# Twelve of 22 gate and up pairs of each FFN from seven block products, and the FFN in three blocks

## The chip, the cores and the metric

The kernel runs on one core of a Trainium2 chip, in one launch. The metric is the device time of that launch in microseconds. TensorE (PE) does the matrix products; its weight loads (PEld) are listed apart from its products. VectorE (DVE), ScalarE (ACT) and GpSimd (POOL) work element by element, and SyncE (SP) issues the loads of the weights from memory.

## The reference

One decoder layer on 512 tokens of width D = 1024, all in fp32. Its first and its last stage are the same kind of feed-forward network (FFN), each with its own weights; the token mixers and a cross-attention between them are not touched by the change.

```python
def swiglu(u, w_gate_up, w_down):
    gate, up = jnp.split(u @ w_gate_up, 2, axis=-1)
    return (jax.nn.silu(gate) * up) @ w_down

h = h + 0.5 * swiglu(rmsnorm(h, g1), w_gu1, w_d1)     # w_gate_up: 1024 x 5632, w_down: 2816 x 1024
...                                                   # mixers, cross-attention
h = h + 0.5 * swiglu(rmsnorm(h, g2), w_gu2, w_d2)
out = rmsnorm(h, g_final)
```

The width of the FFN, 2816, is 22 chunks of 128 (KF = 22); the width of the model is 8 chunks (KD = 8).

## The kernel before

All values lie transposed: 128 features of a chunk on the partitions, the 512 tokens along the row. A product of one 128x128 block of weights with a chunk's 512 tokens is one accumulation step. To keep fp32's accuracy, each fp32 operand is held as two numbers of the faster type fp32r, a rounded one ("hi") and the rest ("lo"), and each step is three products: hi by hi (L114), hi by the tokens' lo (L115), the weights' lo by hi (L116). `split` makes the two: ScalarE casts (L88), then VectorE subtracts (L89).

`load_w` brings 1024 columns of weights (eight blocks of 128) with one DMA into `wr` and splits them into `wh` and `wl`; each of the three names is a ring of three buffers. `job(pt, w, xs)` loads the weights of one output chunk and runs its products into one PSUM tile: 24 of them for eight input chunks, 66 (three loads of 1024, 1024 and 768 columns) for 22. PSUM has five buffers `pj` for such outputs and three `ss` for small things.

`ffn` goes over the 22 chunks `ct`. For each it runs two jobs, one for the gate (`pg`) and one for the up projection (`pu`), 48 products of 512 tokens. Then VectorE multiplies `pg` by the norm's factor `r` (L181), ScalarE takes silu (L182), VectorE multiplies by `pu` (L183), and the result is split into `sh` and `sl`, which stay for all 22 chunks. After the 22nd come eight down jobs of 66 products over all of them; each is scaled (L197) and added to `h` (L199). In the second FFN the last down job is `finish`: in two halves of 256 tokens it does the 66 products (L654 to L656), the final norm, the transposes and the output's DMA.

The tokens' own factors are `uh` and `ul` (`gained`, L123 and L124: h times the norm's gain, split). The order of the instructions on each engine comes from a scheduler that works from the order of the code, and each engine then runs its list in that order, waiting where a semaphore is not there yet.

Of the kernel before, what the change touches and what calls it, by code (L numbers as in the profile page):

```python
# [46 lines left out]
def layer(ctx: ExitStack, tc: tile.TileContext, a, out):  # L48
# [120 lines left out]

    def ffn(gname, wgu, wd, fin=None):  # L170
        with tc.tile_pool(name=nm("fp"), bufs=1, reuse_waits="tile") as fp:
            u = [gained(h[k], gname, k, up) for k in range(KD)]
            s = []
            for ct in range(KF):
                pg, pu = ps(), ps()
                job(pg, wgu[ct], u)
                job(pu, wgu[KF + ct], u)
                if ct == 0:
                    r = rms(h, D, wk)
                gt = fp.tile([P, T], F32, tag="gt", name=nm("gt"), bufs=2)  # L180
                V.tensor_tensor(out=gt, in0=pg, in1=r, op=ALU.mult)  # L181
                S.activation(out=gt, in_=gt, func=AF.Silu)  # L182
                V.tensor_tensor(out=gt, in0=pu, in1=gt, op=ALU.mult)  # L183
                hi = fp.tile([P, T], F32R, tag=f"sh{ct}", name=nm("sh"))
# [567 lines left out]
```

## Time and profile before

| | us |
|---|---|
| median of 3 runs | 1611.11 |
| lowest and highest | 1610.34, 1614.96 |
| the profiled execution, its own time | 1613.93 |
| its span in the trace | 1612.2 |
| TensorE busy in it | 1583.2 (98%) |
| weight loads busy | 1305.2 (81%) |
| VectorE busy | 853.6 (53%) |
| ScalarE busy | 660.3 (41%) |

The span is what the trace covers; the execution's own time is 1.7 us more, for what lies around it. "Busy" sums the instructions of an engine; weight loads run beside products. The two FFNs take the stretches from the start to about 370 us and from about 1180 us to the end.

### The profile page before, as it was taken

To read this page: it belongs to the slowest core of one execution; us is meant where nothing else is said; L and a number is where in the kernel's file an instruction comes from. 1 tells how busy PE (TensorE), PEld (TensorE's weight loads), DVE (VectorE), ACT (ScalarE), POOL (GpSimd) and SP (SyncE) were. 2 spreads that over 40 slices of the span, in tenths; PEclk is the share of its full clock that TensorE was granted. 3 is DMA by queue.
4 is the path that set the end of the run, shared out by engine and by line. 5 is a ranking of instruction groups with operands and counts; after the bars stand their busy time and mean duration, and the time that the engine had idled before them with its cause. 6 is when DMAs were issued, how large, how long until landed. Compare 5 with 4: busy or idle time off the path is not lost.

```text
span 1612.2 us, 18647 instructions
## 1 busy us (share of the span) xinstructions
PE 1583.2 (98%) x7437; PEld 1305.2 (81%) x7437; DVE 853.6 (53%) x1134; ACT 660.3 (41%) x888; POOL 50.8 (3%) x54
## 2 busy tenths in 40 slices
PE   8999999999999999999999999999999999999997
PEld 6888888887878787787888888888888888888887
DVE  5434343346695877858564544555555434443333
ACT  6223232225778493765332223344443323222222
POOL 0000000000120100201010000000000000000000
PEclk9999999999999999999999999999999999999999
DMA  5332323333442323333253233335213233332331
GB/s 194 94 103 91 103 91 104 115 108 105 126 131 78 125 85 122 114 95 109 85 185 102 92 104 93 94 107 178 79 32 113 92 100 96 94 103 86 95 98 62
DMA packets 53911, 168.58 MB, mean 105 GB/s; under 512 B 6320, under 2 KB 6832, under 8 KB 53824
## 3 DMA queue, kind: packets, MB, share of 16 engines
q1 hardware_dynamic: 51952, 161.03, 32.2%
q0 software_dynamic: 1584, 5.31, 0.9%
q8 instruction: 58, 0.95, 0.2%
q10 hardware_dynamic: 288, 1.05, 0.2%
q14 instruction: 29, 0.24, 0.0%
HBM read 163.10 MB, written 4.26 MB: 104 GB/s over the span
## 4 chain that ended last, share of the span: by engine, by line
PE 57%; issue 1%; DVE 1%; ACT 0%; DMA 0%; DVEq 0%; ACTq 0%
PE pj L114 17%; PE pj L116 17%; PE pj L115 17%; PE pj L520 0%; PE pj L521 0%; PE pj L522 0%; PE ss L383 0%; PE pj L654 0%; PE pj L656 0%; PE pj L655 0%; PE ss L388 0%; DMA m<-acd 0%; PE ss L602 0%; PE ss L565 0%; PE ss L564 0%
## 5 line engine op out<-in xcount | busy, mean ns | idle before, releaser
L88 ACT CAST wh<-wr 128x1024 fp32r<-128x1024 f32 (+2 forms) x298 | 294.3, 988 | 794.2 <-PE pj L115 667.8
L114 PE MATMUL pj<-uh,wh 128*128 128x512 f32 x1416 | 556.4, 393 | 7.0 <-ACT wh L88 7.0
L116 PE MATMUL pj<-uh,wl 128*128 128x512 f32 x1416 | 554.9, 392 | 0.0
L115 PE MATMUL pj<-ul,wh 128*128 128x512 f32 x1416 | 554.3, 392 | 0.0
L89 DVE TENSOR_TENSOR wl<-wr,wh 128x1024 fp32r<-128x1024 f32 (+2 forms) x298 | 341.0, 1145 | 196.9 <-ACT wh L88 190.0
L114 PEld LDWEIGHTS pj<-uh,wh 128*128 128x128 f32 x1416 | 266.6, 188 | 63.2 <-ACT wh L88 7.0
L116 PEld LDWEIGHTS pj<-uh,wl 128*128 128x128 f32 x1416 | 266.5, 188 | 56.9 <-issue 0.7
L115 PEld LDWEIGHTS pj<-ul,wh 128*128 128x128 f32 x1416 | 266.5, 188 | 55.7 <-DVE ul L124 0.7
L114 PE MATMUL pj<-sh,wh 128*128 128x512 f32 x330 | 128.9, 390 | 0.0
L116 PE MATMUL pj<-sh,wl 128*128 128x512 f32 x330 | 128.5, 389 | 0.0
L115 PE MATMUL pj<-sl,wh 128*128 128x512 f32 x330 | 128.5, 389 | 0.0
L183 DVE TENSOR_TENSOR gt<-pj,gt 128x512 f32<-128x512 f32 x44 | 30.4, 691 | 137.2 <-PE pj L116 136.5
L181 DVE TENSOR_TENSOR gt<-pj,r 128x512 f32<-128x512 f32 x44 | 30.3, 691 | 113.0 <-PE pj L116 109.5
L116 PEld LDWEIGHTS pj<-sh,wl 128*128 128x128 f32 x330 | 61.9, 188 | 12.9
L114 PEld LDWEIGHTS pj<-sh,wh 128*128 128x128 f32 x330 | 62.0, 188 | 12.7
L115 PEld LDWEIGHTS pj<-sl,wh 128*128 128x128 f32 x330 | 62.0, 188 | 12.7
L225 DVE SCALAR_TENSOR_TENSOR cv<-cx,prm,cv 128x511 f32<-128x511 f32 (+2 forms) x72 | 63.3, 883 | 3.3 <-ACT cv L222 3.0
L366 POOL TENSOR_TENSOR m<-m,keep 128x512 f32<-128x512 f32 x32 | 40.4, 1277 | 309.9 <-DMA m<-acd 297.6
L116 PE MATMUL pj<-ynh,wl 128*128 128x512 f32 x128 | 49.8, 389 | 0.0
L115 PE MATMUL pj<-ynl,wh 128*128 128x512 f32 x128 | 49.8, 389 | 0.0
L114 PE MATMUL pj<-ynh,wh 128*128 128x512 f32 x128 | 49.8, 389 | 0.0
L138 DVE TENSOR_TENSOR sq<-sq,sq 128x512 f32<-128x512 f32 (+1 forms) x47 | 31.2, 665 | 2.5 <-ACT sq L134 1.8
(223 smaller groups left out, 1661.6 us busy)
## 6 DMA issues: line engine op xcount, KB each, us to landing
wr<-in_w_gu SPq DMA_DIRECT2D x87, 512.0 KB, 3.5
wr<-in_w_in SPq DMA_DIRECT2D x80, 512.0 KB, 3.6
wr<-in_w_d SPq DMA_DIRECT2D x32, 512.0 KB, 3.5
m<-acd SPq DMA_DIRECT2D x32, 256.0 KB, 3.9
wr<-in_w_os SPq DMA_DIRECT2D x32, 256.0 KB, 3.0
wr<-in_w_d SPq DMA_DIRECT2D x16, 384.0 KB, 3.1
ea<-acd SPq DMA_DIRECT2D x32, 128.0 KB, 4.1
wr<-in_w_oa SPq DMA_DIRECT2D x8, 512.0 KB, 3.5
```

The lines of the kernel that those rows point to most:

```text
L88: S.copy(out=hi, in_=src)
L89: V.tensor_tensor(out=lo, in0=src, in1=hi, op=ALU.subtract)
L114: TE.matmul(pt, hi[:, s_], xh, start=(k == 0), stop=False)
L115: TE.matmul(pt, hi[:, s_], xl, start=False, stop=False)
L116: TE.matmul(pt, lo[:, s_], xh, start=False, stop=(k == nk - 1))
L138: V.tensor_tensor(out=sq, in0=acc, in1=sq, op=ALU.add)
L181: V.tensor_tensor(out=gt, in0=pg, in1=r, op=ALU.mult)
L183: V.tensor_tensor(out=gt, in0=pu, in1=gt, op=ALU.mult)
L225: V.scalar_tensor_tensor(out=acc[:, d:], in0=x[:, :T - d], scalar=pc(wname, j0 + j), in1=acc[:, d:], op0=ALU.mult, op1=ALU.add)
L366: G.tensor_tensor(out=m4, in0=m4, in1=acs[:, (h0 + hh) * NC:(h0 + hh + 1) * NC].unsqueeze(2) .to_broadcast([P, NC, P]), op=ALU.subtract)
```

## The change

`ffn` works in three blocks of chunks (SB = 8: chunks 0 to 7, 8 to 15, 16 to 21). Each block is followed by the eight down jobs over its own chunks alone (24, 24 and 18 products each), so `h` is scaled and added to three times instead of once, and `sh` and `sl` are kept for eight chunks.

In each FFN 12 of the 22 chunks (`seven`: 4, 5, 7, 8, 10, 11, 13, 14, 16, 17, 19, 20) get their gate and up projections by Strassen's scheme. The weights of a pair are seen as four blocks (a, c: gate and up over input chunks 0 to 3; b, d: over chunks 4 to 7), the tokens as two halves of 256 times two groups of input chunks, and seven products of such blocks replace eight. Each has four input chunks and 256 tokens, so 12 products of 256 columns: 7 x 12 = 84 products of 256 columns in place of 48 of 512. `seven_a` runs four of the seven (48 products, L212 to L215 in `mm3`), `seven_b` the other three (36), one chunk later in the code. The remaining ten chunks (`plain`) are computed as before.

Around them: `_pairs` packs the weights of a pair in the new order on the host, so the two DMAs of a pair remain 1024 columns each. VectorE forms sums of weight blocks (`s31` in two halves, `ca` in place, `s4`: 512 columns each), and the splits of a pair are three of 1024 columns (`w31`, `w2a`, `wdb`) and one of 512 (`w4`). `token_sums`, once in an FFN behind chunk 1, forms the four sums of token blocks and splits them into `th` and `tl`. At the output, ScalarE copies two halves out of PSUM into `ev` and VectorE adds (L291 and its like), then forms `xx` (L304 to L307) and `gt` (L311, L312). OFF and the tile `lag` shift the places in the local memory of some tiles: read from the built programs, the tokens of a product start at the same address modulo 512 bytes as its weights in nearly all products of before, and 192 bytes past it in the seven-product pairs.

```diff
 NC = 4
 EPS = 1e-6
+def seven(ct):
+    return ct >= 4 and ct % 3 != 0
...
+    def ring(tag, dt=F32R):
+        return wp.tile([P, 1024], dt, tag=tag, name=nm(tag), bufs=3)
...
-    first.append(load_w(a["w_gu1"][KF][:, :8 * P], 8 * P))
+    first.append(load_w(a["w_gu1"][0][:, 8 * P:], 8 * P))
...
     def ffn(gname, wgu, wd, fin=None):
-        with tc.tile_pool(name=nm("fp"), bufs=1, reuse_waits="tile") as fp:
-            u = [gained(h[k], gname, k, up) for k in range(KD)]
-            s = []
-            for ct in range(KF):
-                pg, pu = ps(), ps()
-                job(pg, wgu[ct], u)
-                job(pu, wgu[KF + ct], u)
-                if ct == 0:
-                    r = rms(h, D, wk)
-                gt = fp.tile([P, T], F32, tag="gt", name=nm("gt"), bufs=2)
-                V.tensor_tensor(out=gt, in0=pg, in1=r, op=ALU.mult)
-                S.activation(out=gt, in_=gt, func=AF.Silu)
-                V.tensor_tensor(out=gt, in0=pu, in1=gt, op=ALU.mult)
-                hi = fp.tile([P, T], F32R, tag=f"sh{ct}", name=nm("sh"))
-                lo = fp.tile([P, T], F32R, tag=f"sl{ct}", name=nm("sl"))
-                split(gt, hi, lo)
-                s.append((hi, lo))
+        fs = ExitStack()
+        fp = fs.enter_context(tc.tile_pool(name=nm("fp"), bufs=1, reuse_waits="tile"))
+        ts = ExitStack()
+        tp = ts.enter_context(tc.tile_pool(name=nm("tp"), bufs=1, reuse_waits="tile"))
+        tp.tile([P, 48], F32, tag="lag", name=nm("lag"))
+        u = [gained(h[k], gname, k, up) for k in range(KD)]
+        tq = []
+        s = {}
+        def split_pair(src):
+            ws = [fp.tile([P, 1280], F32R, tag=t, name=nm(t), bufs=2) for t in ("xh", "xl")]
+            split(src.rearrange("p (a n) -> p a n", a=2),
+                  *(t[:, :2 * (512 + OFF)].rearrange("p (a n) -> p a n", a=2)[:, :, :512]
+                    for t in ws))
+            return ws
+        def mm3(pt, w, off, xs, start, stop):
+            hi, lo = w
+            for k in range(4):
+                c = slice(off + k * P, off + (k + 1) * P)
+                xh, xl = xs[k]
+                TE.matmul(pt, hi[:, c], xh, start=start and k == 0, stop=False,
+                          skip_group_check=True)
+                TE.matmul(pt, hi[:, c], xl, start=False, stop=False, skip_group_check=True)
+                TE.matmul(pt, lo[:, c], xh, start=False, stop=stop and k == 3,
+                          skip_group_check=True)
+        def quad(k0, i):
+            c = slice(i * H, (i + 1) * H)
+            return [(u[k0 + k][0][:, c], u[k0 + k][1][:, c]) for k in range(4)]
+        def tsum(i):
+            c = slice(i * H, (i + 1) * H)
+            return [(x[0][:, c], x[1][:, c]) for x in tq]
+        def token_sums():
+            for k in range(4):
+                x = wk.tile([P, T], F32, tag="sq", name=nm("ug"), bufs=3)
+                y = wk.tile([P, T], F32, tag="sq", name=nm("ug"), bufs=3)
+                S.activation(out=x, in_=h[k], func=AF.Copy, scale=pc(gname, k))
+                S.activation(out=y, in_=h[k + 4], func=AF.Copy, scale=pc(gname, k + 4))
+                q = fp.tile([P, 1024], F32, tag="sa", name=nm("tq"), bufs=2)
+                V.tensor_tensor(out=q[:, 0:H], in0=x[:, 0:H], in1=x[:, H:], op=ALU.subtract)
+                V.tensor_tensor(out=q[:, H:2 * H], in0=y[:, H:], in1=x[:, H:], op=ALU.subtract)
+                V.scalar_tensor_tensor(out=q[:, 2 * H:3 * H], in0=q[:, 0:H], scalar=-1.0,
+                                       in1=y[:, H:], op0=ALU.mult, op1=ALU.subtract)
+                V.scalar_tensor_tensor(out=q[:, 3 * H:], in0=q[:, 2 * H:3 * H], scalar=-1.0,
+                                       in1=y[:, 0:H], op0=ALU.mult, op1=ALU.subtract)
+                hi = tp.tile([P, 4 * H], F32R, tag=f"th{k}", name=nm("th"))
+                lo = tp.tile([P, 4 * H], F32R, tag=f"tl{k}", name=nm("tl"))
+                split(q, hi, lo)
+                tq.append((hi, lo))
+        def act(ct, g, uv, sign):
+            S.activation(out=g, in_=g, func=AF.Silu)
+            if sign > 0:
+                V.tensor_tensor(out=g, in0=uv, in1=g, op=ALU.mult)
+            else:
+                V.scalar_tensor_tensor(out=g, in0=uv, scalar=-1.0, in1=g, op0=ALU.mult,
+                                       op1=ALU.mult)
+            hi = fp.tile([P, T], F32R, tag=f"sh{ct % SB}", name=nm("sh"))
+            lo = fp.tile([P, T], F32R, tag=f"sl{ct % SB}", name=nm("sl"))
+            split(g, hi, lo)
+            s[ct] = (hi, lo)
+        def plain(ct):
+            pu, pg = ps(), ps()
+            for i in range(2):
+                w = load_w(wgu[ct][:, i * 1024:(i + 1) * 1024], 1024)
+                mm3(pu, w, 0, u[4 * i:4 * i + 4], i == 0, i == 1)
+                mm3(pg, w, 512, u[4 * i:4 * i + 4], i == 0, i == 1)
+            return pu, pg
+        def plain_out(ct, pu, pg):
+            g = fp.tile([P, T], F32, tag="gt", name=nm("gt"), bufs=2)
+            V.tensor_tensor(out=g, in0=pg, in1=r, op=ALU.mult)
+            act(ct, g, pu, 1)
+        def seven_a(ct):
+            ca = ring("wr", F32)
+            db = fp.tile([P, 1024], F32, tag="db", name=nm("db"), bufs=2)
+            nc.sync.dma_start(out=ca, in_=wgu[ct][:, :1024])
+            nc.sync.dma_start(out=db, in_=wgu[ct][:, 1024:])
+            c, a_, d, b = ca[:, :512], ca[:, 512:], db[:, :512], db[:, 512:]
+            s31 = fp.tile([P, 1024], F32, tag="sa", name=nm("sa"), bufs=2)
+            V.tensor_tensor(out=s31[:, 512:], in0=c, in1=d, op=ALU.add)
+            V.tensor_tensor(out=s31[:, :512], in0=c, in1=a_, op=ALU.add)
+            w31 = ring("wh"), ring("wl")
+            split(s31, *w31)
+            V.tensor_tensor(out=c, in0=a_, in1=s31[:, 512:], op=ALU.add)
+            w2a = split_pair(ca)
+            s4 = fp.tile([P, 512], F32, tag="sb", name=nm("sb"), bufs=2)
+            V.tensor_tensor(out=s4, in0=c, in1=b, op=ALU.add)
+            A, B = ps(), ps()
+            mm3(B[:, 0:H], w31, 512, tsum(0), True, True)
+            mm3(B[:, H:], w31, 0, tsum(1), False, True)
+            ev = fp.tile([P, T], F32, tag="ev", name=nm("ev"), bufs=2)
+            S.copy(out=ev[:, 0:H], in_=B[:, 0:H])
+            V.tensor_tensor(out=ev[:, 0:H], in0=B[:, H:], in1=ev[:, 0:H], op=ALU.add)
+            mm3(A[:, 0:H], w2a, 512 + OFF, quad(0, 0), True, True)
+            mm3(A[:, H:], w2a, 0, tsum(2), False, True)
+            S.copy(out=ev[:, H:], in_=A[:, H:])
+            V.tensor_tensor(out=ev[:, H:], in0=A[:, 0:H], in1=ev[:, H:], op=ALU.add)
+            return ct, A, B, ev, s4, db
+        def seven_b(ct, A, B, ev, s4, db):
+            w4 = ring("wh"), ring("wl")
+            split(s4, *(t[:, OFF:OFF + 512] for t in w4))
+            wdb = split_pair(db)
+            mm3(B[:, 0:H], w4, OFF, quad(4, 1), False, True)
+            mm3(B[:, H:], wdb, 0, tsum(3), False, True)
+            mm3(A[:, 0:H], wdb, 512 + OFF, quad(4, 0), False, True)
+            x = fp.tile([P, 768], F32, tag="xx", name=nm("xx"), bufs=1)
+            V.tensor_tensor(out=x[:, 2 * H:3 * H], in0=ev[:, 0:H], in1=ev[:, H:], op=ALU.add)
+            V.tensor_tensor(out=x[:, 0:2 * H].rearrange("p (a t) -> p a t", a=2),
+                            in0=B.rearrange("p (a t) -> p a t", a=2),
+                            in1=ev[:, H:].unsqueeze(1).to_broadcast([P, 2, H]), op=ALU.add)
+            g = fp.tile([P, T], F32, tag="gt", name=nm("gt"), bufs=2)
+            V.tensor_tensor(out=g[:, 0:H], in0=A[:, 0:H], in1=r[:, 0:H], op=ALU.mult)
+            V.tensor_tensor(out=g[:, H:], in0=x[:, 0:H], in1=r[:, H:], op=ALU.mult)
+            act(ct, g, x[:, H:3 * H], -1)
+        for b0 in range(0, KF, SB):
+            b1 = min(KF, b0 + SB)
+            wait = None
+            for ct in range(b0, b1):
+                if seven(ct):
+                    nxt = seven_a(ct)
+                    if wait is not None:
+                        seven_b(*wait)
+                    wait = nxt
+                else:
+                    p = plain(ct)
+                    if ct == 0:
+                        r = rms(h, D, wk)
+                    plain_out(ct, *p)
+                    if wait is not None:
+                        seven_b(*wait)
+                        wait = None
+                if ct == 1:
+                    token_sums()
+            if wait is not None:
+                seven_b(*wait)
+            sb = [s[ct] for ct in range(b0, b1)]
+            last = fin is not None and b1 == KF
+            if b1 == KF:
+                ts.close()
+            if last:
+                op = fs.enter_context(tc.tile_pool(name=nm("op"), bufs=1, reuse_waits="tile"))
             for ct in range(KD):
-                if fin is not None and ct == KD - 1:
-                    fin(fp, wd[ct], s, r)
+                w = wd[ct][:, b0 * P:b1 * P]
+                if last and ct == KD - 1:
+                    fin(fp, w, sb, r)
                     break
                 pd = ps()
-                job(pd, wd[ct], s)
-                if fin is not None and ct > 0:
-                    emit(fp, ct - 1)
+                job(pd, w, sb)
...
+        ws = [load_w(w[:, k0 * P:min(nk, k0 + per) * P], (min(nk, k0 + per) - k0) * P)
+              for k0 in range(0, nk, per)]
         ov = out.rearrange("(c p) f -> c p f", p=P)
         sd = small("sdf", 8, 1)
         for half in range(2):
...
+def _pairs(w):
+    c = _chunks(w)
+    g, u = c[:KF], c[KF:]
+    return np.ascontiguousarray(np.concatenate(
+        [u[:, :, :512], g[:, :, :512], u[:, :, 512:], g[:, :, 512:]], axis=2))
...
```

The first place is VectorE's list in the FFN, within one pair of before (`wl` is the lo of weights, `sl` that of an output).

```order
L181 TENSOR_TENSOR gt_799<-pj_737,r_237 128x512 [waits PE_49]
L89 TENSOR_TENSOR wl_841<-wr_839,wh_840 128x1024 [waits DMAHW7_49,Activation_49]
L183 TENSOR_TENSOR gt_799<-pj_738,gt_799 128x512 [waits PE_49,Activation_49]
L89 TENSOR_TENSOR wl_881<-wr_879,wh_880 128x1024 [waits DMAHW0_49,Activation_49]
L89 TENSOR_TENSOR sl_804<-gt_799,sh_803 128x512 [waits Activation_49]
```

The same engine now, from the last split of chunk 10's first half to the outputs of chunks 9 and 8 (`sa`, `sb`: sums of weights; L104, L268 and L249 are L89, L181 and L183 of before).

```order
L104 TENSOR_TENSOR wl_1449<-sa_1445,wh_1448 128x1024 [waits PE_49,Activation_49]
L268 TENSOR_TENSOR gt_1377<-pj_1316,r_241 128x512 [waits PE_49]
L104 TENSOR_TENSOR wl_1522<-sa_1518,wh_1521 128x1024 [waits Activation_49]
L249 TENSOR_TENSOR gt_1377<-pj_1315,gt_1377 128x512 [waits Activation_49]
L104 TENSOR_TENSOR wl_1588<-sb_1457,wh_1587 128x512 [waits PE_49,Activation_49]
L307 TENSOR_TENSOR xx_1429<-pj_1261,ev_1286 128x512 [waits PE_49]
L104 TENSOR_TENSOR sl_1382<-gt_1377,sh_1381 128x512 [waits Activation_49]
L311 TENSOR_TENSOR gt_1432<-pj_1260,r_241 128x256 [waits PE_49]
L312 TENSOR_TENSOR gt_1432<-xx_1429,r_241 128x256 [waits DVE_49]
L104 TENSOR_TENSOR xl_1527<-wr_1514,xh_1526 128x2x512 [waits Activation_49]
```

Five instructions a pair were all there was; now sums, splits from `sa`, `sb` and `wr`, and pieces of outputs of two chunks alternate, and each waits in its turn.

The second place is TensorE's list at the hand-over from one job to the next in an FFN, before.

```order
L114 MATMUL pj_808<-uh_144,wh_840 128x512
L115 MATMUL pj_808<-ul_145,wh_840 128x512
L116 MATMUL pj_808<-uh_144,wl_841 128x512
L114 MATMUL pj_877<-uh_116,wh_880 128x512 [waits Activation_49]
L115 MATMUL pj_877<-ul_117,wh_880 128x512
L116 MATMUL pj_877<-uh_116,wl_881 128x512 [waits DVE_49]
```

Now the hand-over from chunk 8's last product block to chunk 10's first (`pj_1260` is chunk 8's A, `pj_1460` chunk 10's B).

```order
L212 MATMUL pj_1260<-uh_148,xh_1389 128x256
L214 MATMUL pj_1260<-ul_149,xh_1389 128x256
L215 MATMUL pj_1260<-uh_148,xl_1390 128x256
L212 MATMUL pj_1460<-th_330,wh_1448 128x256 [waits Activation_49]
L214 MATMUL pj_1460<-tl_331,wh_1448 128x256
L215 MATMUL pj_1460<-th_330,wl_1449 128x256 [waits DVE_49]
```

The two waits stand at the same steps as before, for the cast and for the subtraction, but the weights behind them are sums (`sa`) that VectorE has made first, and the steps are 256 columns long.

The third place is TensorE's list where the first down job comes to the newest chunk's output, before (the last three of 66 products, then the next job).

```order
L114 MATMUL pj_1717<-sh_1643,wh_1779 128x512
L115 MATMUL pj_1717<-sl_1644,wh_1779 128x512
L116 MATMUL pj_1717<-sh_1643,wl_1780 128x512
L114 MATMUL pj_1717<-sh_1713,wh_1779 128x512 [waits Activation_49]
L115 MATMUL pj_1717<-sl_1714,wh_1779 128x512 [waits DVE_49]
L116 MATMUL pj_1717<-sh_1713,wl_1780 128x512
```

Now in block 2 (the products 16 to 21 of 24 of its first down job; `sh_2093` is chunk 14's output).

```order
L130 MATMUL pj_2097<-sh_1967,wh_2099 128x512
L131 MATMUL pj_2097<-sl_1968,wh_2099 128x512
L132 MATMUL pj_2097<-sh_1967,wl_2100 128x512
L130 MATMUL pj_2097<-sh_2093,wh_2099 128x512 [waits Activation_49]
L131 MATMUL pj_2097<-sl_2094,wh_2099 128x512 [waits DVE_49]
L132 MATMUL pj_2097<-sh_2093,wl_2100 128x512
```

Before, 63 products stood ahead of the wait for the last output; now 18 do, and such a place comes three times in an FFN.

## Rows read from the trace of the kernel before

**Rows 1.** The page: busy time by engine, and TensorE and its clock in 40 slices.

```profile
PE 1583.2 (98%) x7437; PEld 1305.2 (81%) x7437; DVE 853.6 (53%) x1134; ACT 660.3 (41%) x888; POOL 50.8 (3%) x54
...
PE   8999999999999999999999999999999999999997
...
PEclk9999999999999999999999999999999999999999
```

**Rows 2.** Busy time of each engine in a stretch of either FFN.

```profile
core 0: us, PE busy (x) PEld busy (x) DVE busy (x) ACT busy (x) POOL busy (x), PEclk, DMA share, GB/s
45.00:350.00 305.00, 305.00 (x1347) 252.59 (x1346) 122.83 (x140) 87.71 (x109) 3.41 (x6) 1.00 0.33 101
1180.00:1480.00 300.00, 299.91 (x1355) 247.86 (x1354) 134.99 (x173) 100.96 (x142) 0.00 (x0) 1.00 0.29 89
```

**Rows 3.** Timeline of TensorE in the first FFN: start, duration, instruction; 97 starts apart.

```profile
199.97 0.39 PE L114 MATMUL pj<-uh,wh 128*128 128x512 f32 x1
...
221.95 0.39 PE L115 MATMUL pj<-ul,wh 128*128 128x512 f32 x1
```

**Rows 4.** Groups of TensorE by form: count, busy, mean ns, idle before.

```profile
L114 PE MATMUL pj<-uh,wh 128*128 128x512 f32 x1408 | 553.2, 393 | 7.0 <-ACT wh L88 7.0
...
L114 PE MATMUL pj<-sh,wh 128*128 128x512 f32 x330 | 128.9, 390 | 0.0
```

**Rows 5.** Timeline of TensorE in `finish`, products of 256 columns; 63 starts apart.

```profile
1585.40 0.28 PE L656 MATMUL pj<-sh,wl 128*128 128x256 f32 x1
...
1592.95 0.28 PE L656 MATMUL pj<-sh,wl 128*128 128x256 f32 x1
```

**Rows 6.** Timeline of TensorE: chains of 128 columns, eight and four products.

```profile
433.45 1.05 PE L303 MATMUL ss<-ct,bt 128*128 128x128 f32 x8
...
434.66 0.60 PE L321 MATMUL ss<-con,xs 128*128 128x128 f32 x4
```

**Rows 7.** Timeline of TensorE in the 32-column job `w_dt`; 17 starts apart.

```profile
370.64 0.39 PE L114 MATMUL pj<-uh,wh 128*32 128x512 f32 x1
...
374.56 0.39 PE L116 MATMUL pj<-uh,wl 128*32 128x512 f32 x1
```

**Rows 8.** Groups of VectorE by form.

```profile
L89 DVE TENSOR_TENSOR wl<-wr,wh 128x1024 fp32r<-128x1024 f32 x247 | 302.0, 1223 | 175.7 <-ACT wh L88 168.8 <-PE ss L303 1.5
L183 DVE TENSOR_TENSOR gt<-pj,gt 128x512 f32<-128x512 f32 x44 | 30.4, 691 | 137.2 <-PE pj L116 136.5 <-ACT gt L182 0.7
...
L89 DVE TENSOR_TENSOR sl<-gt,sh 128x512 fp32r<-128x512 f32 x44 | 30.1, 684 | 0.7 <-ACT sh L88 0.7
...
L124 DVE SCALAR_TENSOR_TENSOR ul<-h,prm,uh 128x512 fp32r<-128x512 f32 x16 | 11.6, 749 | 11.2 <-ACT uh L123 11.2
...
L509 DVE TENSOR_TENSOR kl<-pj,kh 128x256 fp32r<-128x256 f32 x8 | 3.3, 417 | 0.0
```

**Rows 9.** Timeline of VectorE at the start, instructions queued one behind the other.

```profile
14.91 1.48 DVE L138 TENSOR_TENSOR sq<-sq,sq 128x512 f32<-128x512 f32 x2
16.31 1.22 DVE L89 TENSOR_TENSOR wl<-wr,wh 128x1024 fp32r<-128x1024 f32 x1
17.45 1.48 DVE L138 TENSOR_TENSOR sq<-sq,sq 128x512 f32<-128x512 f32 x2
...
27.82 1.29 DVE L181 TENSOR_TENSOR gt<-pj,r 128x512 f32<-128x512 f32 x2 [1.40 <-ACT r L154]
```

**Rows 10.** Groups of ScalarE by form.

```profile
L88 ACT CAST wh<-wr 128x1024 fp32r<-128x1024 f32 x247 | 259.6, 1051 | 700.0 <-PE pj L115 580.6 <-issue 96.2 <-PE pj L116 11.7
L182 ACT ACTIVATE gt<-gt 128x512 f32<-128x512 f32 x44 | 27.8, 634 | 0.5 <-DVE gt L181 0.5
L88 ACT CAST sh<-gt 128x512 fp32r<-128x512 f32 x44 | 27.3, 621 | 0.5 <-DVE gt L183 0.2
...
L508 ACT CAST kh<-pj 128x256 fp32r<-128x256 f32 x8 | 2.9, 366 | 0.0
```

**Rows 11.** DMA issues of the gate and up weights: count, KB, us to landing.

```profile
wr<-in_w_gu SPq DMA_DIRECT2D x87, 512.0 KB, 3.5
```

**Rows 12.** Timeline of VectorE and ScalarE behind `finish`'s first half.

```profile
1593.27 0.42 DVE L660 SCALAR_TENSOR_TENSOR dn<-pj,r 128x256 f32<-128x256 f32 x1 [4.32 <-PE pj L656]
1593.72 0.42 DVE L662 TENSOR_TENSOR hb<-dn,hb 128x256 f32<-128x256 f32 x1
...
1594.19 0.42 ACT L664 ACTIVATE sq<-hb 128x256 f32<-128x256 f32 x1
```

More of the change, by code (lines that the diff above doesn't have):

```diff
@@ L32 @@
 MB = 4
+OFF = 80
+SB = 8
 PJ = 5
@@ L188, in ffn @@
             for ct in range(KD):
-                if fin is not None and ct == KD - 1:
-                    fin(fp, wd[ct], s, r)
+                w = wd[ct][:, b0 * P:b1 * P]
+                if last and ct == KD - 1:
+                    fin(fp, w, sb, r)
                     break
                 pd = ps()
-                job(pd, wd[ct], s)
-                if fin is not None and ct > 0:
-                    emit(fp, ct - 1)
+                job(pd, w, sb)
+                if last and ct > 0:
+                    emit(op, ct - 1)
@@ L199, in ffn @@
                 V.tensor_tensor(out=h[ct], in0=dn, in1=h[ct], op=ALU.add)
+        fs.close()
     ffn("ffn1_norm", a["w_gu1"], a["w_d1"])
@@ L643, in finish @@
         per = 8
-        ws = [load_w(w[:, k0 * P:min(KF, k0 + per) * P], (min(KF, k0 + per) - k0) * P)
-              for k0 in range(0, KF, per)]
+        nk = len(s)
+        ws = [load_w(w[:, k0 * P:min(nk, k0 + per) * P], (min(nk, k0 + per) - k0) * P)
+              for k0 in range(0, nk, per)]
         ov = out.rearrange("(c p) f -> c p f", p=P)
@@ L650, in finish @@
             pd = ps()
-            for k in range(KF):
+            for k in range(nk):
                 hi, lo = ws[k // per]
@@ L655, in finish @@
                 TE.matmul(pd[:, :256], hi[:, c], s[k][1][:, hs], start=False, stop=False)
-                TE.matmul(pd[:, :256], lo[:, c], s[k][0][:, hs], start=False, stop=(k == KF - 1))
+                TE.matmul(pd[:, :256], lo[:, c], s[k][0][:, hs], start=False, stop=(k == nk - 1))
             if half == 0:
@@ L729 @@
             [np.repeat(x["ssm_dt_bias"][0], NC), np.repeat(x["ssm_a_log"][0], NC)]), (P, 2 * P))),
[L730 removed]
+        "w_gu1": _pairs(x["ffn1_w_gate_up"][0]),
         "w_d1": _chunks(x["ffn1_w_down"][0]),
@@ L740 @@
         "w_o": _chunks(x["w_o_x"][0]),
-        "w_gu2": _chunks(x["ffn2_w_gate_up"][0]),
+        "w_gu2": _pairs(x["ffn2_w_gate_up"][0]),
         "w_d2": _chunks(x["ffn2_w_down"][0]),
     }
-    nc = bacc.Bacc("TRN2", target_bir_lowering=False, num_devices=1)
+    nc = bacc.Bacc("TRN2", target_bir_lowering=False, num_devices=1,
+                   dynamic_dma_scratch_size=8192)
     args = {n: nc.dram_tensor("in_" + n, v.shape, mybir.dt.from_np(v.dtype),
```

6 lines of the change are left out of this document (2 added, 4 removed).

## The prediction

> **What bounds the kernel now.** I read the page first: TensorE is busy for 98% of the span, VectorE for 53%, ScalarE for 41%, and the clock row stands at full speed almost throughout [rows 1]. So time can only come from TensorE doing less, or be lost where it is made to wait. Then the stretches of the FFNs, since the change lies there alone: in 305 us of the first and 300 of the second TensorE has no gap (305.00, 299.91), the granted clock is 1.00, VectorE is at 40 and 45%, ScalarE at 29 and 34%, the DMA engines at a third [rows 2]. The reader should see that no other engine is near its limit, but that VectorE, at 122.83 us in 305, has less than threefold room.
>
> Then the price of a product. An entry lasts 0.39 us [rows 4], but entries overlap; what counts is the distance of starts: (221.95 - 199.97)/97 = 226.6 ns for 512 columns [rows 3], which at 2.4 GHz is 213.3 + 13.3. Products of 256 columns with 128-column weights occur in `finish`: (1592.95 - 1585.40)/63 = 119.8, say 120 ns, which is 106.7 + 13 [rows 5]. So halving the columns does not quite halve the price.
>
> **The change, part by part.**
>
> *Seven products.* A pair costs 48 x 226.6 = 10.877 us before. After, 84 products of 256 columns. At the 120 ns of [rows 5] that is 10.08, 0.80 less. But in [rows 5] tokens and weights start alike modulo 512 bytes, in the new pairs 192 bytes apart, and no row shows that case. Bounds: products of 128 columns, with a weight load each, go at (1.05 - 0.275)/7 = 111 ns where the starts are alike and at (0.60 - 0.275)/3 = 108 where they are 160 bytes apart [rows 6] (0.275 is what one entry lasts past its pitch, from [rows 5]); a 128-column weight load fits into that, and 256 columns take 106.7, so 111 is the floor: 84 x 111 = 9.32. The other way, in `w_dt`, where starts are apart by several amounts and the weights have 32 columns, 512 columns take (374.56 - 370.64)/17 = 230.6, 4 ns more than 226.6 [rows 7]; 120 + 4 = 124 gives 10.42. Nearest in shape is 120; as the 128-column rows gain 3 ns by a shift, I take 117: 9.83 us, 1.05 less a pair, 25.2 for 24 pairs. The ends are 37.3 (111) and 11.1 (124).
>
> The Trainium skill ("TensorE: Matmul & The Clock Gate", Back-to-back issue gap) gives N/2.4 + 2.5 ns for a single gap: 216 and 109 ns, a pair falling from 10.36 to 9.17, which would save 28.4 us, an estimate from that page, against 25.2 here. The rows disagree with it by some 11 ns a product, so it enters no number here.
>
> *Three blocks.* The number of down products is unchanged (8 x 66 an FFN), and so are their columns; they come from the same loads cut otherwise (1024, 1024 and 768 columns). `dn` and the addition to `h` come three times instead of once: 16 more of each an FFN, 2 x 16 x 0.69 = 22 us of VectorE an FFN [rows 8], beside 5.4 us down jobs (24 x 0.2266) that ask VectorE for 1.22 + 1.38: cover enough, nothing on the path.
>
> *Block ends.* The last seven-product pair has a tail before the first down job can use it: 0.32 from the start of the last product to VectorE (1592.95 to 1593.27, [rows 5, 12]), less 0.12 for that product itself, two `gt` halves at 0.42, silu 0.63, the multiplication 0.75, cast 0.62, subtraction 0.68 [rows 8, 10, 12], and four hand-overs of 0.05 (1593.72 + 0.42 to 1594.19, [rows 12]): 3.9 us after the job begins. TensorE gets there, by the third place of the order, after 19 products in block 2: 4.3 us; in block 3, with 14 to 16 products ahead, 3.2 to 3.6. So 0 and some 0.5, and up to 1.05 more in each where a weight's cast [rows 10] stands on ScalarE just when silu is due; I take 0.7 an FFN, 1.4 in all, with 0.6 and 5 as ends. Block 1 ends with plain work in between: nothing. What is late next is only the following down job, whose products the scheduler already draws forward.
>
> *Token sums.* Each FFN pays 4 x (four 256-column sums + one split of 1024) on VectorE at its start, 4 x (4 x 0.42 + 1.22) = 11.6 us, among the work of chunks 1 and 2 with their 1.22 splits behind it in the queue; 8 copies on ScalarE. TensorE needs chunk 2's second weights about 39.6 us in; by my count VectorE delivers them between 38.7 and 40.5. So 0 to 0.9, taken as 0.5, twice: 1.0.
>
> *VectorE's pace.* A seven-product pair asks for eight operations of 512 columns (four sums of weights, `xx`, the multiplication, two splits), three splits of 1024 and five of 256: 8 x 0.69 + 3 x 1.22 + 5 x 0.42 = 11.3 us by durations [rows 8]. Queued instructions start nearer: 1.14 after a 1.22 split (16.31 to 17.45), 0.60 after one of 512 (1.29 for two, less 0.69), so 10.0 us [rows 9]. A plain pair takes 4.1 to 4.5. Of chunks, two of three are of the new kind: 24.1 to 27.1 us of VectorE in 2 x 9.83 + 10.88 = 30.5 us of TensorE, 79 to 89%. It has room on average, so I take nothing, and keep the case that it has none as a rival. ScalarE has some 5.8 us a pair.
>
> [...]
>
> *DMA.* Two loads of 512 KB a pair as before, landing 3.5 us after issue [rows 11] with the DMA engines at a third [rows 2]: nothing.
>
> *Hand-over to the mixers and the end.* The mixers' first splits now follow shorter down jobs: 0.5 (0 to 2), taken from the same tail of 0.69 operations. `finish` has 18 products a half instead of 66, so its first half's tail (norm, output, some 5 us from 1593.27 on) has less cover, +1.0 (0 to 3), against 0.6 that TensorE gains: 132 products of 256 columns cost 0.85 us more than 66 of 512 (15.81 against 14.96), 36 only 0.24 more than 18. Net 0.4.
>
> *Sum.* -25.2 + 1.0 + 1.4 + 0.5 + 0.4 = -21.9. The profiled execution's span is 1612.2, so 1590.3; its own time was 1613.93, 1.7 more than its span: 1592.0. That execution lies 2.8 above the median of 1611.11 (runs 1610.34 to 1614.96); against the median I forecast 1589.
>
> **The rivals.** A measurement of this kernel tells a difference of about 0.3%, 4.8 us, from none.
>
> (a) *The shift of 192 bytes frees the weight load:* pitch at the floor, 111 instead of 117: 12.1 us less, 1577. For it: 120 - 106.7 leaves 13 ns that no column needs, and the shifted row of [rows 6] is the faster. Against: `w_dt` is slower with its mixture [rows 7]. Chance 0.25.
>
> (b) *The shift gains nothing or costs:* 120 or 124 ns: +6.0 or +14.1, 1595 to 1603; or block ends and starts at their upper ends, of a like size. Chance 0.18.
>
> (c) *Buffers of PSUM run short:* each new pair holds two of five buffers from `seven_a` to the end of `seven_b`, one chunk later, and the copies into `ev` and `xx` must read them. If each pair waits 1.0 us for one (a copy of 0.37, an addition of 0.42 and hand-overs), the gain goes: 1589 + 24 = 1613, no change; at eight places, 1597. For it: six PSUM tiles could be alive around a plain chunk. Against: by the order each buffer's last reader stands several us ahead of the next writer. Chance 0.11.
>
> (d) *VectorE paces the pairs, the other side:* it runs its list in order, the rings have two or three buffers, and if plain chunks' room can't be used, a pair takes VectorE's 11.3 us by durations instead of 10.88 before: 24 x (11.29 - 10.88) = +9.9, and the losses of 3.3: 1611 + 13 = 1624, slower. It decides when VectorE's work for three chunks passes TensorE's 30.5 us; 27.1 is the most that rows give, so waits of 1.7 us a seven-product pair inside VectorE's list would do it. For it: outputs of two chunks alternate with splits that wait for ScalarE (order, first place). Chance 0.09.
>
> **How the numbers follow.** The main case (pitch 114 to 118, waits as summed; 1584 to 1594) has 0.37, so 1589. Faster: it, (a) and (b), 0.80; the same: (c), 0.11; slower: (d), 0.09. The range leaves out (c) at full size and (d), and reaches from the floor pitch to rival (b) with a few us of waits more: 1575 to 1606.
>
> **What the profile of after would show.** Distance of starts in a seven-product pair: 117 ns by me, 111 by (a), 120 or more by (b). Idle time of TensorE in the FFN stretches: under 4 us in all by me; if it names `pj` copies or additions of VectorE as releasers at each pair's first product, (c); if the splits `wl` and `xl` end the waits and VectorE stands over 95% in the stretch, (d). VectorE at 79 to 89% between the blocks' ends. The clock should stay at 1.00; a clock that falls behind a wait would add to any of the losses. I am wrong if TensorE's busy time falls by less than 11 us, or if its idle time grows by as much as its busy time falls.

## The result, and the profile after

The changed kernel takes 1592.53 us (median of 4 runs, 1592.52 to 1593.47), the kernel before 1610.91 (4 runs with the one beside it): a ratio of 0.9875, 95% interval 0.9858 to 0.9893 (the two medians divided give 0.9886, inside that interval). The forecast was 1589, with 1575 to 1606 as its range; it was faster, as forecast. The profiled execution took 1592.54 us with a span of 1590.8; the forecast for these two was 1592.0 and 1590.3.

The page of the changed kernel, busy time by engine (answers to [rows 1]):

```profile
PE 1557.4 (98%) x8253; PEld 1318.0 (83%) x8253; DVE 1056.0 (66%) x1502; ACT 733.7 (46%) x1008; POOL 52.7 (3%) x54
```

TensorE is busy for 25.8 us less and VectorE for 202 us more; TensorE still fills 98% of the span. Busy time by stretch (answers to [rows 2]); the third stretch is four pairs by seven products and two plain chunks, without down jobs:

```profile
core 0: us, PE busy (x) PEld busy (x) DVE busy (x) ACT busy (x) POOL busy (x), PEclk, DMA share, GB/s
45.00:340.00 295.00, 294.83 (x1789) 263.03 (x1788) 204.42 (x290) 111.79 (x150) 1.25 (x2) 1.00 0.32 100
1180.00:1470.00 290.00, 289.83 (x1622) 252.28 (x1622) 197.11 (x283) 119.49 (x164) 0.00 (x0) 1.00 0.32 100
...
145.00:206.00 61.00, 61.00 (x438) 57.23 (x437) 45.77 (x69) 27.49 (x39) 0.00 (x0) 1.00 0.33 104
```

TensorE has 0.17 us idle in each of two long stretches, the clock is full, and VectorE stands at 45.77 in 61 us, 75%, among the pairs. It has most to do around the token sums, 31.76 us in 35 or 91%, and there too TensorE has no gap:

```profile
25.00:60.00 35.00, 35.00 (x177) 29.59 (x176) 31.76 (x51) 23.61 (x34) 0.00 (x0) 1.00 0.27 83
```

A list of TensorE's waits between 20 and 365 us holds no entry. So nothing took the place of the work that went; what is left is the price of a product. The timeline of TensorE over two pairs, 168 products in an unbroken row (answers to [rows 3, 5]):

```profile
156.99 0.28 PE L212 MATMUL pj<-uh,wh 128*128 128x256 f32 x1
...
176.33 0.28 PE L215 MATMUL pj<-uh,xl 128*128 128x256 f32 x1
```

19.34 us over 167 starts is 115.8 ns, where [rows 5] gave 119.8 for the same shape: a pair costs 9.73 us. Taken over all 2016 such products of the trace the mean is 116.2 ns, 234.2 us in all. It is a mixture, though each of these products has the same 192 bytes: twelve products by token sums `th`, then twelve by `uh`, in the same row:

```profile
166.73 0.28 PE L212 MATMUL pj<-th,wh 128*128 128x256 f32 x1
...
168.09 0.28 PE L212 MATMUL pj<-th,wh 128*128 128x256 f32 x1
...
169.45 0.28 PE L212 MATMUL pj<-uh,xh 128*128 128x256 f32 x1
...
170.86 0.29 PE L212 MATMUL pj<-th,xh 128*128 128x256 f32 x1
```

1.36/12 is 113.3 ns and 1.41/12 is 117.5. Over the whole trace the products by `th` and `tl` come 115.0 ns apart on average, those by `uh` and `ul` 117.5. What makes the difference was not found.

Where blocks end, TensorE's timeline in blocks 1, 2 and 3 of the first FFN:

```profile
92.67 0.40 PE L131 MATMUL pj<-sl,wh 128*128 128x512 f32 x1
93.08 0.38 PE L212 MATMUL pj<-uh,wh 128*128 128x256 f32 x1
...
226.04 0.39 PE L130 MATMUL pj<-sh,wh 128*128 128x512 f32 x1
226.54 0.50 PE L131 MATMUL pj<-sl,wh 128*128 128x512 f32 x1
226.88 0.40 PE L132 MATMUL pj<-sh,wl 128*128 128x512 f32 x1
...
329.48 0.94 PE L130 MATMUL pj<-sh,wh 128*128 128x512 f32 x2
330.26 0.40 PE L131 MATMUL pj<-sl,wh 128*128 128x512 f32 x1
```

The next start should come 0.23 later. In block 1 it comes after 0.41: 0.2 us lost, at a place where two down products stand between `seven_a` and `seven_b` of chunk 7's pair. In block 2 it comes after 0.50 and 0.34: 0.4 lost; in block 3 two products take 0.78 in place of 0.45: 0.3. In blocks 2 and 3 these places are where TensorE comes to the newest `sh` and `sl`.

### The profile page after: what moved, and what is told of

Its sections match the earlier page's. It is cut to its first block, busy times and chain, and to the rows that moved or that the text cites. A ratio compares the mean times of both kernels' runs of the same rounds, so it can differ in the third digit from the quotient of the medians.

```text
span 1590.8 us, 20744 instructions
## 1 busy us (share of the span) xinstructions
PE 1557.4 (98%) x8253; PEld 1318.0 (83%) x8253; DVE 1056.0 (66%) x1502; ACT 733.7 (46%) x1008; POOL 52.7 (3%) x54
## 4 chain that ended last, share of the span: by engine, by line
PE 55%; DVE 2%; issue 1%; ACT 1%; DMA 0%; DVEq 0%; ACTq 0%
PE pj L132 12%; PE pj L131 12%; PE pj L130 12%; PE pj L212 5%; PE pj L214 5%; PE pj L215 5%; DMA ea<-acd 0%; PE pj L676 0%; PE pj L678 0%; PE pj L677 0%; PE ss L539 0%; DVE wl L104 0%; PE ss L758 0%; ACT wh L103 0%; PE ss L721 0%
## 5 line engine op out<-in xcount | busy, mean ns | idle before, releaser
L104 DVE TENSOR_TENSOR wl<-wr,wh 128x1024 fp32r<-128x1024 f32 (+2 forms) x250 | 282.0, 1129 | 112.6 <-ACT wh L103 111.0
L130 PE MATMUL pj<-uh,wh 128*128 128x512 f32 (+1 forms) x712 | 281.2, 395 | 0.0
L132 PE MATMUL pj<-uh,wl 128*128 128x512 f32 (+1 forms) x712 | 280.4, 394 | 0.0
L131 PE MATMUL pj<-ul,wh 128*128 128x512 f32 (+1 forms) x712 | 279.5, 393 | 0.0
L212 PE MATMUL pj<-uh,wh 128*128 128x512 f32 (+1 forms) x416 | 153.3, 369 | 8.3 <-ACT wh L103 7.1
L132 PEld LDWEIGHTS pj<-uh,wl 128*128 128x128 f32 (+1 forms) x712 | 133.9, 188 | 29.0 <-issue 0.7
L130 PEld LDWEIGHTS pj<-uh,wh 128*128 128x128 f32 (+1 forms) x712 | 133.8, 188 | 28.6 <-issue 0.9
L131 PEld LDWEIGHTS pj<-ul,wh 128*128 128x128 f32 (+1 forms) x712 | 134.0, 188 | 27.8
L214 PE MATMUL pj<-ul,wh 128*128 128x512 f32 (+1 forms) x416 | 152.4, 367 | 0.0
L215 PE MATMUL pj<-uh,wl 128*128 128x512 f32 (+1 forms) x416 | 151.9, 366 | 0.0
L212 PEld LDWEIGHTS pj<-uh,wh 128*128 128x128 f32 x416 | 78.6, 189 | 22.6 <-ACT wh L103 7.1
L214 PEld LDWEIGHTS pj<-ul,wh 128*128 128x128 f32 x416 | 79.0, 190 | 13.1 <-DVE ul L140 0.5
L215 PEld LDWEIGHTS pj<-uh,wl 128*128 128x128 f32 x416 | 78.5, 189 | 12.8 <-DVE wl L104 0.2
```

Source lines behind the costliest of these rows:

```text
L104: V.tensor_tensor(out=lo, in0=src, in1=hi, op=ALU.subtract)
L130: TE.matmul(pt, hi[:, s_], xh, start=(k == 0), stop=False)
L131: TE.matmul(pt, hi[:, s_], xl, start=False, stop=False)
L132: TE.matmul(pt, lo[:, s_], xh, start=False, stop=(k == nk - 1))
L212: TE.matmul(pt, hi[:, c], xh, start=start and k == 0, stop=False, skip_group_check=True)
L214: TE.matmul(pt, hi[:, c], xl, start=False, stop=False, skip_group_check=True)
```

## The experiments

They ran later than the first result, with medians of 1613.9 to 1614.7 for the kernel before, so each is told by its ratio to the kernel before on the same chip (4 runs or more, 95% interval).

**1. The blocks without the products.**

```diff
 def seven(ct):
-    return ct >= 4 and ct % 3 != 0
+    return False
```

> No pair by seven products; the three blocks, the packed weights and token_sums (whose results then serve nothing) stay. Theory (all of the gain is TensorE's work saved in the 24 pairs, the rest costs or brings about a microsecond): about 1610 to 1613 us, no difference from before. Rival (the blocks bring part of the gain, since the last job of the kernel is 36 products of 256 columns and not 132, and the kernel ends sooner after it): 1600 to 1605 us.

Measured: 1.0021 (1.0007 to 1.0034), some 3 us slower than before. The blocks, the packed weights and the token sums bring nothing; they cost a little. All of the gain is in the 24 pairs.

**2. The 192 bytes.** The first two kernels change OFF and `lag` and nothing else; the first of them:

```diff
-OFF = 80
+OFF = 0
...
-        tp.tile([P, 48], F32, tag="lag", name=nm("lag"))
```

> OFF is 0 and the lag tile is gone, so tokens and weights of the seven-product pairs start alike modulo 512 bytes, as in all products of before; nothing else changes. Theory (the gain is the number of products times the distance of their starts, and the 192 bytes give part of it): the distance goes from the 116 ns that the changed kernel shows back to the 120 ns of the rows of before, 2016 products x 3.6 ns = +7.3 us, 1600 us. Rival (the shift does nothing, the pairs' distance is what it is for another reason): 116 ns and 1592.5 us.

Measured: 0.9926 (0.9912 to 0.9941), 0.5% or some 8 us behind the changed kernel's 0.9875. The same stretch of TensorE's timeline (one line is gone from the kernel, so L211 and L214 are L212 and L215):

```profile
157.12 0.28 PE L211 MATMUL pj<-uh,wh 128*128 128x256 f32 x1
...
177.16 0.28 PE L214 MATMUL pj<-uh,xl 128*128 128x256 f32 x1
```

20.04/167 = 120.0 ns, as in [rows 5], and so is the mean of all 2016 products; against 116.2 that is 2016 x 3.8 ns = 7.7 us. The theory holds, the rival falls.

> As the changed kernel, with 128 bytes between tokens and weights modulo 512 in place of 192 (OFF 96, lag 32). Theory (the shift sets the distance of starts, by its size): a distance between 116 and 120 ns, 1592 to 1600 us. Rival (any shift serves alike): 116 ns, 1592.5 us.

Measured (OFF 96, lag 32): 0.9906 (0.9889 to 0.9922).

```profile
158.34 0.29 PE L212 MATMUL pj<-uh,wh 128*128 128x256 f32 x1
...
178.22 0.29 PE L215 MATMUL pj<-uh,xl 128*128 128x256 f32 x1
```

119.0 ns: a shift as such does not do it. Two more, on the kernel of experiment 4 (18 chunks, whose ratio with 192 bytes is 0.9766), with 256 bytes (OFF 64, lag 64) and 224 (OFF 72, lag 56):

> 18 of 22 chunks, ring of three for db, with 256 bytes between tokens and weights in place of 192 (OFF 64, lag 64). Distance of starts with 0 bytes 120 ns, with 128 some 119, with 192 some 116. Theory (it goes on falling with the distance): below 116 ns, down to the 111 of the rows with 128 columns, so 3024 products x up to 5 ns = up to 15 us less than with 192. Rival (192 is a best place, or bytes count by another pattern): 116 to 124 ns, the same to 24 us more.

> 18 of 22 chunks, ring of three for db, 224 bytes between tokens and weights (OFF 72, lag 56). So far: 0 and 256 bytes 120 ns, 128 some 119, 192 some 116. Theory (the pattern repeats after 256 bytes and has its low between 128 and 256, with 192 near it): 116 to 119 ns, 0 to 8 us more than with 192. Rival (the low lies between 192 and 256): 111 to 115 ns, 4 to 15 us less than with 192.

Measured: 0.9828 (0.9806 to 0.9849) with 256 and 0.9811 (0.9782 to 0.9841) with 224. TensorE's timelines over 672 products in a row, with 192, 256 and 224 bytes:

```profile
137.96 0.28 PE L212 MATMUL pj<-th,wh 128*128 128x256 f32 x1
...
215.82 0.28 PE L215 MATMUL pj<-uh,xl 128*128 128x256 f32 x1
```

```profile
139.85 0.28 PE L212 MATMUL pj<-th,wh 128*128 128x256 f32 x1
...
220.37 0.28 PE L215 MATMUL pj<-uh,xl 128*128 128x256 f32 x1
```

```profile
139.86 0.28 PE L212 MATMUL pj<-th,wh 128*128 128x256 f32 x1
...
219.16 0.28 PE L215 MATMUL pj<-uh,xl 128*128 128x256 f32 x1
```

671 starts apart: 116.0, 120.0 and 118.2 ns. My theory that the distance goes on falling was wrong, and so was the rival of a low beyond 192; of the places tried 192 is the best, and 256 is as bad as 0.

The same shift for products of 512 columns, in the kernel before:

```diff
     up = ctx.enter_context(tc.tile_pool(name="up", bufs=1))
+    up.tile([P, 48], F32, tag="lag", name=nm("lag"))
...
-    nc = bacc.Bacc("TRN2", target_bir_lowering=False, num_devices=1)
+    nc = bacc.Bacc("TRN2", target_bir_lowering=False, num_devices=1, dynamic_dma_scratch_size=8192)
```

> The kernel before with one dummy tile of 48 floats ahead of the tokens' tiles, so that tokens and weights start 192 bytes apart modulo 512 in nearly all products of 512 columns too (and a smaller scratch space for GpSimd's DMAs, which gives the room). Theory (the shift frees a few ns of each product only where 13 ns of a weight load stand out past 256 columns; at 512 the same 13 ns are there in 226.6 = 213.3 + 13.3, so they may shrink alike): 223 ns a product, 6900 x 3.6 = 25 us less than before. Rival (at 512 columns the shift does nothing, or costs the 4 ns of the w_dt rows): no change, or 28 us more.

Measured: 1.0228 (1.0200 to 1.0255), 37 us slower. TensorE's timeline, 96 starts apart:

```profile
200.09 0.39 PE L115 MATMUL pj<-ul,wh 128*128 128x512 f32 x1
...
222.49 0.39 PE L115 MATMUL pj<-ul,wh 128*128 128x512 f32 x1
```

22.40/96 = 233.3 ns in place of 226.6 [rows 3]. What helps at 256 columns by 4 ns costs 6.7 at 512: my theory had the wrong sign there, and the rival, with the `w_dt` rows, the right one, though it said 28 us. The same execution shows both signs at once, for the mixers have a job of 256 columns, which this kernel shifts by the same 192 bytes. Its starts before (168 products) and now (188 products):

```profile
1078.04 0.29 PE L115 MATMUL pj<-mnl,wh 128*128 128x256 f32 x1
...
1098.07 0.28 PE L116 MATMUL pj<-mnh,wl 128*128 128x256 f32 x1
```

```profile
1102.62 0.28 PE L116 MATMUL pj<-mnh,wl 128*128 128x256 f32 x1
...
1123.83 0.28 PE L116 MATMUL pj<-mnh,wl 128*128 128x256 f32 x1
```

20.03/167 = 119.9 ns before and 21.21/187 = 113.4 with the shift. So within one execution the sign goes with the width. Why it turns was not found.

**3. More pairs by seven products.**

```diff
-    return ct >= 4 and ct % 3 != 0
+    return ct >= 4
```

> All chunks from 4 on by seven products, 18 of 22 in each FFN, so no plain chunk lies between two of them. Theory (TensorE alone sets the time): 12 more pairs save 12 x 1.1 = 13 us, 1579 us. Rival (VectorE's list becomes the pace once plain chunks give it no room): by queued starts 10.0 us a pair against TensorE's 9.8, so 36 x 0.2 = 8 us come back, 1587 us; by full durations 11.3 us, 36 x 1.5 = 55 us come back, 1634 us. TensorE's idle time in the FFNs then ends on VectorE's splits, and VectorE is busy for over 95% of blocks 2 and 3.

Measured: 1.0122 (1.0103 to 1.0141), 20 us slower than before, with less work for TensorE. By the numbers the rival of full durations was right (1633.69 measured, 1634 said), but not its mechanism. A stretch of some six such pairs and nothing else, by windows:

```profile
145.00:222.00 77.00, 67.77 (x527) 65.09 (x526) 58.96 (x94) 33.24 (x50) 0.00 (x0) 0.95 0.23 76
```

TensorE is idle for 9.2 of 77 us and the granted clock falls to 0.95, but VectorE is at 77%, not at 95, and the DMA engines rest more than in the changed kernel. Its waits in the first FFN:

```profile
PE pj L212 <- ACT wh L103: 11.0, 8, 3.2
PE pj L215 <- DVE wl L104: 2.4, 5, 0.8
PE pj L212 <- ACT xh L103: 1.3, 3, 0.4
```

They end on casts of weights. Followed back through the timelines of VectorE, SyncE, VectorE again, ScalarE and TensorE:

```profile
198.20 1.22 DVE L104 TENSOR_TENSOR xl<-db,xh 128x1024 fp32r<-128x1024 f32 x1
...
199.48 0.33 SPq L275 DMA_DIRECT2D db<-in_w_gu  x1
...
203.17 0.69 DVE L278 TENSOR_TENSOR sa<-wr,db 128x512 f32<-128x512 f32 x1 [2.27 <-DMA db<-in_w_gu]
...
203.90 1.05 ACT L103 CAST wh<-sa 128x1024 fp32r<-128x1024 f32 x1 [3.46 <-DVE sa L278]
...
205.00 0.38 PE L212 MATMUL pj<-th,wh 128*128 128x256 f32 x1 [0.76 <-ACT wh L103]
```

The split of an old `db` ends at 199.42 and its buffer comes free; the load for the pair after next is issued at 199.48 and lands at 203.17; only then can VectorE form the sum (it idles 2.27 us for it), ScalarE cast and TensorE begin. With two buffers this chain is part of each pair's round where no plain chunk stands between. The next run tests that.

**4. A third buffer for `db`**, with the 18 chunks. GpSimd's scratch space is halved, which makes the room.

```diff
-            db = fp.tile([P, 1024], F32, tag="db", name=nm("db"), bufs=2)
+            db = fp.tile([P, 1024], F32, tag="db", name=nm("db"), bufs=3)
...
-                   dynamic_dma_scratch_size=8192)
+                   dynamic_dma_scratch_size=4096)
```

> As the run with 18 of 22 chunks by seven products, with a ring of three buffers for db in place of two (and a smaller scratch space for GpSimd's DMAs, which gives the room). Theory (there the second load of a pair could be issued only when the split of db two pairs earlier had been done, landed some 4 us later and held up VectorE's sum, the cast and TensorE's first product; VectorE itself was idle for a fifth of the time): with the third buffer the waits go, and what is left is VectorE's 10.0 us a pair against TensorE's 9.8: 1580 to 1595 us. Rival (VectorE's list as such is too long or too strictly ordered for pairs without a plain chunk between them): the waits stay, 1620 us or more.

Measured: 1577.08 us, 0.9766 (0.9747 to 0.9785), the fastest kernel of this study. Eight pairs in a row, by windows:

```profile
138.00:216.00 78.00, 78.00 (x674) 78.00 (x673) 70.69 (x112) 41.33 (x61) 0.00 (x0) 1.00 0.33 109
```

No idle time and full clock, with VectorE at 91%: 8.8 us a pair, less than the 10.0 I had counted by queued starts. The ring was the cause, unless the smaller scratch space helped. The next run has both, the third buffer and the smaller space, with the change's own 12 chunks:

> The changed kernel with its 12 of 22 chunks, but a ring of three buffers for db (and the smaller scratch space), as the run with 18 chunks had. Theory (with a plain chunk between two pairs of new ones the second buffer comes free in time, so the ring binds only where there is none): no difference from the changed kernel, ratio to before 0.985 to 0.989. Rival (the third buffer or the scratch space itself saves time, and so part of what the 18 chunks gained is theirs): ratio 0.980 or less.

Measured: 0.9863 (0.9837 to 0.9888), no difference from the changed kernel's 0.9875: with a plain chunk after each two, the second buffer comes free in time, and neither the buffer nor the space saves time by itself.

Two chunks further (`ct >= 2`, ring of three):

> All chunks from 2 on by seven products, 20 of 22, ring of three for db. Theory (TensorE's work is what counts while buffers suffice): 4 more pairs than with 18 save 4.4 us, but the first of them needs the token sums right behind chunk 1, and VectorE has some 12 us of them to do while TensorE works off what is left of chunk 1: 3 to 6 us of waiting in each FFN, so ratio 0.975 to 0.982, no better than 18. Rival (the sums are hidden there too): ratio 0.974 or less.

Measured: 0.9856 (0.9831 to 0.9882): worse than 18. The first pair now comes before the token sums have left VectorE. VectorE, ScalarE and TensorE at chunk 2, from the last token sum on, and a window around them:

```profile
40.53 0.42 DVE L238 SCALAR_TENSOR_TENSOR tq<-tq,ug 128x256 f32<-128x256 f32 x1
40.87 0.69 DVE L278 TENSOR_TENSOR sa<-wr,db 128x512 f32<-128x512 f32 x1
...
42.19 1.05 ACT L103 CAST wh<-sa 128x1024 fp32r<-128x1024 f32 x1 [0.16 <-DVE sa L279]
...
43.28 0.58 PE L212 MATMUL pj<-th,wh 128*128 128x256 f32 x1 [8.39 <-ACT wh L103]
```

```profile
25.00:60.00 35.00, 25.67 (x167) 23.41 (x166) 32.12 (x54) 22.90 (x32) 0.00 (x0) 0.85 0.19 66
```

VectorE is busy for 32.12 of 35 us; it can form the pair's first sum of weights (`sa`) only when the last token sum (`tq`) is done, ScalarE casts that sum at 42.19, and TensorE waits 8.39 at once, after which the clock is low for a while (0.85 over the stretch). The direction was foreseen; the wait was more than the 3 to 6 us said.

**5. More work for VectorE** in the changed kernel: the sum `s4` formed four and seven times over, with the same result.

```diff
-            V.tensor_tensor(out=s4, in0=c, in1=b, op=ALU.add)
+            for _ in range(4):
+                V.tensor_tensor(out=s4, in0=c, in1=b, op=ALU.add)
```

> As the changed kernel, but the last sum of weights of a seven-product pair (s4, 512 columns) is formed four times over, the same result each time: three more operations of VectorE a pair, 1.8 us by queued starts, so some 27.7 us of VectorE in the 30.4 us that TensorE takes for three chunks. Theory (VectorE has room): no more than 2 us slower, 1592 to 1595 us on the chip of the first run. Rival (VectorE's ordered list is already at its edge, and what is put into it is passed on): 24 x 1.8 = 43 us slower.

> The same sum formed seven times over: six more operations of VectorE a pair, 3.6 us, so 31.3 us of VectorE by queued starts (34 by durations) in 30.4 us of TensorE. Theory (VectorE decides when its work for three chunks passes TensorE's): it now decides, some 1 to 4 us lost for each three chunks, 8 to 32 us in the 8 groups, and more where the clock falls behind the waits: 1600 to 1630 us. Rival (buffers and loads decide, not VectorE's sum): no difference from the run with three more.

Measured: 0.9861 (0.9843 to 0.9878) and 0.9850 (0.9830 to 0.9871), both the same as the changed kernel. The stretch 145 to 206 with four and with seven sums:

```profile
145.00:206.00 61.00, 61.00 (x436) 57.22 (x436) 51.44 (x78) 27.52 (x39) 0.00 (x0) 1.00 0.32 103
```

```profile
145.00:206.00 61.00, 61.00 (x437) 57.23 (x436) 58.38 (x92) 27.28 (x39) 0.00 (x0) 1.00 0.27 91
```

VectorE goes from 75 to 84 and 96%, and TensorE does not lose a tenth of a microsecond. Three more were expected to be free, and were. Six more were expected to cost 8 us at least: that was wrong, because VectorE's work was overcounted (31.3 us for three chunks; 58.38 x 30.4/61 = 29.1 by the window). Neither run fills its list past 96%, so what a longer one would do is not shown.

## Why the prediction held

*The pairs.* I took 117 ns a product between bounds of 111 and 124, and 25.2 us for 24 pairs. The trace has 116.2 on average, so 24 x 10.877 - 234.2 = 26.8. That the 192 bytes shorten the distance is borne out by experiment 2: without them it is 120. But I had read it from four products of 128 columns, 160 bytes apart [rows 6], and at 512 columns the same shift costs 6.7 ns, so that it held at 256 is in part luck. The Trainium skill gives N/2.4 + 2.5 ns for an isolated gap ("TensorE: Matmul & The Clock Gate", Back-to-back issue gap); an estimate from it is 109 ns here. No row of 256 columns comes that near: the nearest are the 113.3 and 113.4 ns shown above. (By that page the saving works out at 28.6 us, not the 28.4 of the prediction.)

*The losses.* Block ends were taken at 0.7 an FFN, and blocks 2 and 3 lose that. Block 1 was put at nothing because plain work would stand in between. That was misread: its last chunk, 7, is a pair, two down products stand within it, and 0.2 an FFN are lost there. That makes 1.8 in all, for 1.4 taken. `finish` and the tail were taken at +0.4: from its first product to the span's end it is 27.1 us before (1585.08 to 1612.2) and 16.6 after (1574.15 to 1590.8), and 96 products fewer at 0.1198 are 11.5 of that, so the tail costs 1.04, less 0.6 that TensorE gained, +0.4. The token sums were taken at 1.0 and cost nothing: TensorE has no wait there. For the hand-over to the mixers (0.5) no wait shows either.

Three things were not foreseen. The first few products of 512 columns after a row of 256 start up to 236 ns apart in place of 227, which sums to 0.4 an FFN. At the start the cast of the first weights waited for its DMA (TensorE's second group of products began at 9.94, with 1.19 idle), and the 49th product starts 1.3 us later than before (22.35 against 21.10). The mixers, where no work was changed, take 1.1 more (from `w_dt` to the second FFN 866.2 us before, 867.3 after). The last two come and go between executions (0.04 us idle at the start in the run with shift 0, 1.23 in that with 128; the mixers take 865.2 to 869.5 in the profiled executions), so they do not belong to the change. The tail moves in the same way: from the first product of `finish` to the end it is 16.5 in one profiled execution and 18.5 in another, with the same 36 products.

With all of these the sum is -26.8 + 1.8 + 0.4 + 0.8 + 1.3 + 1.1 = -21.4, which is what the span changed by. That the forecast of -21.9 came within 0.5 of it is partly luck: the pairs gave 1.6 more than forecast and two losses of 1.5 did not come, and 3.6 of others, 2.4 of them of that execution alone, stood against them.

*The median.* The span was forecast to 0.5 us and the execution's own time too (1592.0 and 1592.54), the median only to 3.5. The step that missed is the last one: I took the 21.9 us off a median of three executions, 1611.11, which lies 2.8 below the profiled one of before. Whether those three were quick or the profiled one slow is not shown. In the later runs the kernel before has medians of 1613.9 to 1614.7, near the profiled 1613.93, and three kernels with the same pairs (the third buffer with 12 chunks and the two of experiment 5) lie 22.3 to 23.3 below it; that speaks for a quick median, on other chips.

*The rivals.* (a), the floor of 111 ns: not reached, by no shift; single blocks of products come to 113.3. (b): no; 120 ns is what 0 and 256 bytes give. (c), PSUM's buffers: no wait on them anywhere in the FFNs. (d), VectorE's pace: not in this kernel. Its work for three chunks was put at 24.1 to 27.1 us; by the window it is 45.77 x 30.4/61 = 22.8, and experiment 5 shows that its list can be filled to 96% without a wait reaching TensorE. What the rival had right is that plain chunks between the pairs are needed: experiment 3 is as slow as it said, through the ring of two for `db`, not VectorE's rate. The loads, costed at nothing, cost nothing only because of those plain chunks: "two loads of 512 KB a pair as before" left out that the second now waits for a buffer of its own ring.

## What to carry to other kernels

On an engine that is busy for 98% of the time, count products and take the distance of starts from a row of the very shape; then ask for the operands' addresses as well, since 192 bytes were worth 8 us here and 37 the other way. When a stretch with less work becomes slower, look at who is idle: here neither TensorE nor VectorE nor the DMA engines were full, a buffer came free late, and one more buffer turned 20 us lost into 37 gained. A forecast from one profiled execution that is held against a median of three or four can miss by the scatter of both, here by 3 us.

## What the runs showed of the hardware

The distance of starts of fp32r products changes with the place of tokens and weights relative to each other (counted here modulo 512 bytes), and differently by width. With 256 columns, in rows of the seven-product pairs: 120.0 ns at 0 and at 256 bytes, 119.0 at 128, 118.2 at 224, 116.0 at 192; in the mixers 119.9 at 0 and 113.4 at 192. With 512 columns: 226.6 at 0, 233.3 at 192. These bytes are not all that counts: at the same 192, single blocks of the pairs go at 113.3 and at 117.5. The duration that a timeline prints for one entry hardly tells: 0.28 or 0.29 us in all of the former, 0.39 in both of the latter. Only places tried here are listed; the mechanism was not found.
